# Output projections of a two-layer decoder trunk: four column groups, and two pairs of column groups computed as seven block products

## The chip, the cores and the metric

The kernel runs on one core of a Trainium2 chip. The metric is the device time of one execution in microseconds. Times are compared as medians of several executions; where the text argues from a profile, it uses the one execution that the hardware profiler recorded.

The engines go by short names: PE is TensorE (matrix products; PEld its weight loads), DVE is VectorE, ACT is ScalarE, POOL is GpSimd. SP issues most transfers; each issuing engine has its own queue of instructions and works it off in order.

## The reference, cut to what matters

Each of two layers normalises x (512 tokens, 2048 features, float32), projects it to 6656 columns, mixes tokens in three branches (retention, differential attention, RG-LRU with a convolution), multiplies each by a gate, and projects the 2048 mixed features back:

```python
for l in range(DEPTH):                       # DEPTH = 2
    h = rms_norm(x, pre_norm_g[l])
    proj = jnp.einsum('bsd,de->bse', h, w_in[l])
    (rq, rk, rv, rg, dq, dk, dv, dg, lx, lg) = jnp.split(proj, split_idx, axis=-1)
    ...
    lru_out = rg_lru(lx, ...) * jax.nn.silu(lg)
    mixed = jnp.concatenate([ret_out, diff_out, lru_out], axis=-1)
    y = jnp.einsum('bse,ed->bsd', mixed, w_out[l])
    x = x + rms_norm(y, post_norm_g[l])
```

## The kernel before

All large products keep nearly float32 precision by splitting each operand into a high part (`hi`, rounded to the fast matmul format) and the rest (`lo`), and adding three matmuls: hi x hi, hi x lo, lo x hi. The activations' parts stay on the chip (`hhi`/`hlo` for the normalised x, `mhi`/`mlo` for mix, one pair per 128 features). The weights come from DRAM in chunks of 256 rows x 512 columns (512 KB): `load_chunk` (lines 154 to 166) loads `raw` through SP's queue, rounds it to `whi` on ACT (line 164) and subtracts to get `wlo` on DVE (line 165). There are three buffers of each (`WBUFS`), and `ensure` asks for chunks two ahead of their use.

A pass (`run_pass`, lines 191 to 232) is one group of 512 columns: 8 chunks, 4 banks of results (`big`, in PSUM), 2 x 3 matmuls of 512 columns for each chunk and bank (line 209), 192 in all. The last two chunks are taken bank by bank, so that results come out one after another. There are 13 input passes a layer, in forms A (weights stationary, features come out on the partitions) and B (activations stationary, tokens come out on the partitions). The output projection is four passes of form B over `WO[0]` to `WO[3]`; the last runs as two half passes of two token blocks each, with its weights loaded twice.

Token mixing is written as generators in a list (`side`); `pump` takes one step of the first generator after every second group of matmuls. So the order of the code is the order in which each engine's queue is filled; loads and splits are put some way ahead by a priority, and every engine then works its queue in order. Among the generators are `diff_final`, `ret_final` and `lru_final`, which write `mhi` and `mlo`, and the LRU gates `lg`/`lgs` (lines 661 to 667). Six kinds of 512-column products (lines 633, 643, 666, 736, 818, 931) run on POOL.

`evac_y` (lines 787 to 811) takes a result bank of the output projection: a sum of squares on ACT, a product with `pg` (post-norm gain) on DVE. With the fourth group it forms the norm's factor (`sy`, then `ry` by a power on POOL) and calls `finish` (lines 813 to 836): y x ry + `xr`, where `xr` is the residual read again from DRAM. In layer 0 the result goes to `xs` in DRAM and is transposed for the next layer (`hT`, `hhi`, `hlo`); in layer 1 it is the output.

## Time and profile before

| | us |
|---|---|
| median of 3 runs | 1642.38 (1642.27 to 1642.62) |
| the profiled execution | 1641.9 |
| its span | 1640.1 |
| output projection of layer 0, first to last large matmul | about 639 to 820 |
| output projection of layer 1 | about 1458 to 1631 |
| end of the last matmul to the end of the span | 8.8 |

A line of the profile's groups has the line of the kernel, the engine, the operation, result <- operands by the program's names, the shape, the count, then busy time and mean duration in ns, then the engine's idle time just ahead of these instructions and what ended it. Matmuls overlap, so that their durations add up to more than their time. A line of the chain has start, length, engine and what. The rows that carry the argument stand in the prediction.

### The profile page before, as it was taken

What the parts mean: (1) busy time and instruction counts of PE and PEld (TensorE: products, weight loads), DVE (VectorE), ACT (ScalarE), POOL (GpSimd) and SP (SyncE); (2) the same over time, 40 slices, a digit from 0 to 9 for tenths busy, and PEclk for the clock granted to TensorE, in tenths of its full rate; (3) what the DMA queues carried; (4) which work ended last, traced back from release to release, by engine and by line L of the source; (5) the groups of instructions that cost most, each with busy time, mean ns of one, the idle gap of its engine ahead of it and who ended that gap; (6) DMA issues with size and microseconds to landing.
All of it is one profiled execution on the core that took longest, in us unless ns stands there. A gap on an engine that the chain in (4) does not pass through costs nothing.

```text
span 1640.1 us, 19400 instructions
## 1 busy us (share of the span) xinstructions
PE 1623.5 (99%) x7541; PEld 1342.6 (82%) x7541; DVE 902.8 (55%) x1506; ACT 656.5 (40%) x1024; POOL 133.1 (8%) x136
## 2 busy tenths in 40 slices
PE   9999999999999999999999999999999999999997
PEld 7888888888888888888788888887888888888885
DVE  7747756556477444323762774656756644443236
ACT  7233345456633223222752343435662222332233
POOL 1010001001100120000120000101110001100003
PEclk9999999999999999999999999999999999999999
...
GB/s 229 123 97 103 91 103 55 95 77 97 84 97 102 79 65 96 97 185 135 212 154 97 97 94 93 67 82 78 104 84 96 98 64 83 92 103 97 212 122 193
DMA packets 54748, 177.51 MB, mean 108 GB/s; under 512 B 6656, under 2 KB 7680, under 8 KB 54656
## 3 DMA queue, kind: packets, MB, share of 16 engines
...
q14 instruction: 33, 0.27, 0.1%
q10 hardware_dynamic: 144, 0.04, 0.0%
...
## 4 chain that ended last, share of the span: by engine, by line
PE 93%; DVE 3%; issue 2%; ACT 1%; POOL 1%; DMA 0%; DVEq 0%; POOLq 0%; ACTq 0%
PE big L209 86%; PE gate L622 1%; DVE wlo L165 1%; PE acc L515 1%; PE ro L709 1%; PE rs L684 1%; PE ro L712 0%; PE kv L698 0%; PE sc L483 0%; PE sc L482 0%; PE wT L505 0%; ACT whi L164 0%; PE hT L828 0%; DVE y L820 0%; PE rT L739 0%
## 5 line engine op out<-in xcount | busy, mean ns | idle before, releaser
L165 DVE TENSOR_TENSOR wlo<-raw,whi 128x1024 fp32r<-128x1024 f32 (+1 forms) x289 | 354.5, 1230 | 447.8 <-ACT whi L164 441.3
L164 ACT CAST whi<-raw 128x1024 fp32r<-128x1024 f32 (+1 forms) x289 | 302.4, 1048 | 599.9 <-PE big L209 487.3
L209 PE MATMUL big<-hhi,whi 128*128 128x512 f32 x1024 | 402.0, 393 | 0.5 <-DVE lg L663 0.5
L209 PE MATMUL big<-hlo,whi 128*128 128x512 f32 x1024 | 399.1, 390 | 0.0
L209 PE MATMUL big<-hhi,wlo 128*128 128x512 f32 x1024 | 398.9, 390 | 0.0
L209 PE MATMUL big<-whi,hhi 128*128 128x512 f32 x640 | 253.1, 398 | 0.7 <-ACT whi L164 0.7
L209 PE MATMUL big<-whi,hlo 128*128 128x512 f32 x640 | 249.7, 390 | 0.0
L209 PE MATMUL big<-wlo,hhi 128*128 128x512 f32 x640 | 249.7, 391 | 0.0
L209 PEld LDWEIGHTS big<-hhi,whi 128*128 128x128 f32 x1024 | 192.4, 188 | 40.6 <-DVE lg L663 0.9
L209 PEld LDWEIGHTS big<-hhi,wlo 128*128 128x128 f32 x1024 | 192.2, 188 | 40.1
L209 PEld LDWEIGHTS big<-hlo,whi 128*128 128x128 f32 x1024 | 192.5, 188 | 39.1
L209 PE MATMUL big<-wlo,mhi 128*128 128x512 f32 x512 | 199.7, 391 | 1.2 <-DVE wlo L165 1.2
L209 PE MATMUL big<-whi,mhi 128*128 128x512 f32 x512 | 199.9, 390 | 0.0
L209 PE MATMUL big<-whi,mlo 128*128 128x512 f32 x512 | 199.8, 390 | 0.0
L209 PEld LDWEIGHTS big<-wlo,hhi 128*128 128x128 f32 x640 | 120.2, 188 | 25.7
L209 PEld LDWEIGHTS big<-whi,hhi 128*128 128x128 f32 x640 | 120.3, 188 | 24.5 <-ACT whi L164 1.3
L209 PEld LDWEIGHTS big<-whi,hlo 128*128 128x128 f32 x640 | 120.4, 188 | 23.8
L209 PEld LDWEIGHTS big<-wlo,mhi 128*128 128x128 f32 x512 | 96.1, 188 | 22.4 <-DVE wlo L165 2.5
L209 PEld LDWEIGHTS big<-whi,mhi 128*128 128x128 f32 x512 | 96.1, 188 | 20.1 <-ACT whi L164 0.4
L209 PEld LDWEIGHTS big<-whi,mlo 128*128 128x128 f32 x512 | 96.1, 188 | 19.4
L491 ACT ACTIVATE pr<-sc,mx 128x128 f32<-128x128 f32 (+3 forms) x64 | 33.2, 524 | 71.8 <-DVE mx L488 71.7
L417 DVE TENSOR_TENSOR rt<-qk,sin_d 32x512 f32<-32x512 f32 x64 | 43.7, 683 | 3.5 <-ACT qk L459 2.5
...
## 6 DMA issues: line engine op xcount, KB each, us to landing
raw<-in_w_in SPq DMA_DIRECT2D x207, 512.0 KB, 3.6
raw<-in_w_out SPq DMA_DIRECT2D x80, 512.0 KB, 3.4
xT<-in_xt SPq DMA_DIRECT2D x16, 256.0 KB, 6.6
xr<-in_x SPq DMA_DIRECT2D x16, 256.0 KB, 5.7
xs<-y POOLq DMA_DIRECT2D x16, 256.0 KB, 3.5
xr<-xs SPq DMA_DIRECT2D x16, 256.0 KB, 5.6
pg<-in_postg SPq DMA_DIRECT2D x8, 256.0 KB, 3.8
out<-y POOLq DMA_DIRECT2D x8, 256.0 KB, 6.0
```

The lines of the kernel that those rows point to most:

```text
L164: last_copy[0] = A.copy(hi[:, a:b, :], raw[:, a:b, :])
L165: V.tensor_tensor(lo[:, a:b, :], raw[:, a:b, :], hi[:, a:b, :], op=ALU.subtract)
L209: T.matmul(ps[b], lhsT=lhsT, rhs=rhs, start=(cnt[b] == 0), stop=(cnt[b] == total - 1))
L417: V.tensor_tensor(t2[b:b + w, :], raw[a:a + w, :], sin[a:a + w, :], op=ALU.mult)
L491: A.activation(p[:, :n], sc[c][:, :n], AF.Exp, bias=mx[:, c:c + 1], scale=0.125, accum_out=sums[:, h:h + 1])
L515: T.matmul(accs[i][:, h * P:(h + 1) * P], lhsT=wt[:, kb * P:(kb + 1) * P], rhs=dv[kb][:, h * P:(h + 1) * P], start=(kb == 0), stop=(kb == i))
L622: T.matmul(ps[:BW, :], lhsT=wt[:BW, cols], rhs=at[:BW, :], start=(n == 0), stop=(n == 2))
L684: T.matmul(ps[:, n * P:(n + 1) * P], lhsT=k[:, n * P:(n + 1) * P], rhs=q[:, n * P:(n + 1) * P], start=True, stop=True)
L709: T.matmul(po[:, n * P:(n + 1) * P], lhsT=sT[:, n * P:(n + 1) * P], rhs=v[:, n * P:(n + 1) * P], start=True, stop=(n == 0))
```

## The change

The four column groups of an output projection are taken as two pairs (`Pair`, `run_pair`). With A the mix (512 tokens x 2048 features) and B the weights of a pair (2048 rows x 1024 columns), both are cut in 2 x 2 blocks, and the four blocks of the result come from seven block products where eight were computed: A11 B11, A12 B21, A22 T4, S4 B22 and S1 T1, S2 T2, S3 T3, with S1 = A21 - A22, S2 = A11 - S1, S3 = A11 - A21, S4 = A12 - S2 and T1 = B11 + B12, T2 = T1 + B22, T3 = B12 + B22, T4 = T2 + B21. One product is four *units* of 12 matmuls of 512 columns (256 rows of weights, two token blocks), so a pair has 28 units, 336 matmuls. `UNITS` and `UNITS_HALF` are the orders of the units in a layer's first and second pair.

The sums of weights: `pair_unit` keeps B11 in tiles `wx` and adds to it on DVE (T1, T2, T4); T3 is formed by a transfer of POOL's that adds to what is in `raw`. The units are staged: load six units ahead of use (`LOAD`), add four ahead (`ADD`), split two ahead (`SPLIT`). The sums of mix (`Sums.make`, 16 per layer): DVE forms `sf` in float32, ACT and DVE split it into `sp` (two buffers), POOL writes it to DRAM (`sums_out`), and SP reads it back as `s` (four buffers) for each pair. They are made chunk by chunk as `mixed` hands over the last of the four tiles that a chunk needs. The results of the products are combined in `evac` on DVE, three of the seven after a copy by ACT (`held`).

Beside this: the input passes stand in another order (the list `seq` below); v and the gates go to DRAM after their pass (`vg`, `dgs`) and are read back for each head through POOL's queue; layer 1's first pass (`HalfPass`) runs in two halves of two token blocks, with its weights loaded twice; all of POOL's 512-column products but `xsq` run on DVE; `pg`, `xr` and two small loads go through POOL's queue in place of SP's; `NU`, the number of general 512-column buffers, is 63 for 77. The host permutes the columns of `w_in` and the rows of `w_out` to suit. The second pair of layer 0 transposes two token blocks at a time (`turn`).

The first place is DVE's queue at the start of layer 0's output projection. Before, at the end of the last input pass (`dgs`, `dod`, `mlo` belong to differential attention) and with the first splits of the output weights:

```order
L564 SCALAR_TENSOR_TENSOR dgs_5075<-big_4687,rstd,dgs_5075 128x512
L570 TENSOR_TENSOR dod_2782<-dod_2782,dgs_5075 128x512
L578 SCALAR_TENSOR_TENSOR mlo_5088<-dT_5082,subg,mhi_5087 128x512
L578 SCALAR_TENSOR_TENSOR mlo_5097<-dT_5091,subg,mhi_5096 128x512
L578 SCALAR_TENSOR_TENSOR mlo_5106<-dT_5100,subg,mhi_5105 128x512
L578 SCALAR_TENSOR_TENSOR mlo_5115<-dT_5109,subg,mhi_5114 128x512
L165 TENSOR_TENSOR wlo_5126<-raw_5124,whi_5125 128x1024
L165 TENSOR_TENSOR wlo_5156<-raw_5154,whi_5155 128x1024
```

And of the change, with the unit S1_T1 of chunk 1 (`wlo_5417`) and, further on, other units' sums and splits (`wx_4880`, `wx_4881`, `wlo_5440`), the last LRU tiles (`lh`) and their low parts:

```order
L217 TENSOR_TENSOR wlo_5417<-wx_4945,whi_5416 128x512
L217 TENSOR_TENSOR wlo_5417<-wx_4946,whi_5416 128x512
L953 TENSOR_TENSOR lh_3074<-lh_3074,lgs_5198 128x512
L953 TENSOR_TENSOR lh_3620<-lh_3620,lgs_5229 128x512
L258 TENSOR_TENSOR wx_4880<-wx_4880,raw_5457 128x512
L258 TENSOR_TENSOR wx_4881<-wx_4881,raw_5457 128x512
L217 TENSOR_TENSOR wlo_5440<-raw_5272,whi_5439 128x1024
L1034 TENSOR_TENSOR mlo_5298<-lh_3074,mhi_5297 128x512
L953 TENSOR_TENSOR lh_3642<-lh_3642,lgs_5248 128x512
L1034 TENSOR_TENSOR mlo_5303<-lh_3620,mhi_5302 128x512
```

Before, only splits follow the last `mlo`, one for each chunk; now splits, weight sums and the last parts of mix stand between each other.

The second place is PE's queue there, in the change. `big_5282` and `big_5289` are the results of A11_B11, `big_5422` and `big_5429` those of S1_T1:

```order
L414 MATMUL big_5422<-wlo_5417,s_5414 128x512
L414 MATMUL big_5422<-whi_5416,s_5414 128x512 x2
L414 MATMUL big_5422<-wlo_5417,s_5414 128x512
L414 MATMUL big_5429<-wlo_5417,s_5414 128x512
L414 MATMUL big_5429<-whi_5416,s_5414 128x512 x2
L414 MATMUL big_5429<-wlo_5417,s_5414 128x512
L414 MATMUL big_5282<-whi_5307,mhi_5297 128x512
L414 MATMUL big_5289<-whi_5307,mhi_5297 128x512
L414 MATMUL big_5282<-whi_5307,mlo_5298 128x512
```

The unit of S1_T1's chunk 1 (operand `s_5414`), and that of chunk 0 before it, now stand ahead of the last unit of A11_B11, which needs the `mlo` of the rows above.

The third place is DVE's queue at the end of layer 1. Before:

```order
L165 TENSOR_TENSOR wlo_12303<-raw_12301,whi_12302 128x1024
L165 TENSOR_TENSOR wlo_12321<-raw_12319,whi_12320 128x1024
L794 SCALAR_TENSOR_TENSOR sy_12345<-ssy,msy 128x1
L797 TENSOR_TENSOR y_12343<-big_12227,pg_12047 128x512
L820 SCALAR_TENSOR_TENSOR y_11469<-y_11469,ry_12347,xr_11845 128x512
L820 SCALAR_TENSOR_TENSOR y_11727<-y_11727,ry_12347,xr_11847 128x512
```

And of the change, with `wlo_13076` the last split of the kernel, and `e` and `held` the results of token blocks 0 and 1:

```order
L217 TENSOR_TENSOR wlo_13056<-wx_12348,whi_13055 128x512
L1093 SCALAR_TENSOR_TENSOR e_12603<-e_12603,ry_13021,xr_12700 128x512
L1069 TENSOR_TENSOR held_12799<-held_12799,pg_12445 128x512
L1093 SCALAR_TENSOR_TENSOR e_12413<-e_12413,ry_13043,xr_12723 128x512
L1091 TENSOR_TENSOR held_12791<-held_12791,xr_12702 128x512
L1093 SCALAR_TENSOR_TENSOR held_12047<-held_12047,ry_13043,xr_12725 128x512
L1093 SCALAR_TENSOR_TENSOR e_12617<-e_12617,ry_13043,xr_12727 128x512
L1091 TENSOR_TENSOR held_12799<-held_12799,xr_12729 128x512
L217 TENSOR_TENSOR wlo_13076<-wx_12367,whi_13075 128x512
L217 TENSOR_TENSOR wlo_13076<-wx_12368,whi_13075 128x512
```

Before, the finishing of token blocks 2 and 3 follows the last split, and that of blocks 0 and 1 stands five splits ahead of it; now seven rows of finishing blocks 0 and 1 stand right ahead of the last split.

The diff, cut to its core:

```diff
-NU = 77
+NU = 63
 WBUFS = 3
+RBUFS = 4
+SBUFS = 4
+PBUFS = 2
+IN_PAIRS = (False, False)
+SPLIT, ADD, LOAD = 2, 4, 6
...
+class Pair:
+    def __init__(self, w1, w2, act, sums, out1, out2, order=None):
+        self.w, self.act, self.sums, self.out = (w1, w2), act, sums, (out1, out2)
+        self.order = order or UNITS
+        self.x, self.kept = {}, {}
...
+A11_B11, A12_B21, S1_T1, S2_T2, S4_B22, S3_T3, A22_T4 = range(7)
+SUM_OF = {S1_T1: 0, S2_T2: 1, S4_B22: 3, S3_T3: 2}
+ALONE = [[(s, c) for c in range(4)] for s in range(7)]
+def _both(s, t):
+    return [(u, c) for c in range(4) for u in (s, t)]
+UNITS = ALONE[A11_B11] + _both(S1_T1, S3_T3) + _both(S2_T2, S4_B22) + _both(A12_B21, A22_T4)
+UNITS_HALF = ALONE[A11_B11] + ALONE[A12_B21] + _both(S1_T1, S3_T3) + _both(S2_T2, S4_B22) + ALONE[A22_T4]
...
+    def two(tag, s, dt=F32):
+        return wp.tile([P, 2, S], dt, tag=tag, name=nm(s), bufs={"raw": RBUFS, "s": SBUFS, "sp": PBUFS}.get(tag, WBUFS))
...
+    def pair_unit(n, p, s, c):
+        w1, w2 = p.w
+        if s == A11_B11:
+            src = p.x[c] = [U("wx"), U("wx")]
+            for kk in range(2):
+                nc.sync.dma_start(src[kk], w1[c][:, kk * S:(kk + 1) * S])
+        elif s == S1_T1:
+            p.kept[c] = load_raw(w2[c])
+        elif s == S2_T2:
+            p.kept[c] = load_raw(w2[c + 4])
+        elif s == A12_B21 or s == A22_T4 and p.order is not UNITS:
+            p.kept[c] = load_raw(w1[c + 4])
+        yield
+        if s in (S1_T1, S2_T2, A22_T4):
+            src = p.x[c]
+            for kk in range(2):
+                V.tensor_tensor(src[kk], src[kk], p.kept[c][:, kk, :], op=ALU.add)
+        elif s == S3_T3:
+            src = p.kept[c]
+            nc.gpsimd.dma_start(src, w2[c + 4].rearrange("p (k c) -> p k c", k=2), accum_op=ALU.add)
+        elif s != A11_B11:
+            src = p.kept[c]
+        yield
+        sums = None
+        if s in SUM_OF:
+            sums = two("s", "s", F32R)
+            nc.sync.dma_start(sums.bitcast(F32), p.sums.dram[SUM_OF[s], c])
+        hi, lo = split_tiles()
+        if isinstance(src, list):
+            for kk in range(2):
+                split(hi[:, kk, :], lo[:, kk, :], src[kk])
+        else:
+            split(hi, lo, src)
+        unit_tiles[n] = hi, lo, sums
...
+    def ensure(i, ahead=True):
+        for step, more in enumerate((LOAD - SPLIT, ADD - SPLIT, 0)):
+            while reached[step] <= min(i + (more if ahead else 0), len(units) - 1):
+                n = reached[step]
+                p, u = units[n]
+                if n not in steps:
+                    steps[n] = pair_unit(n, p, *u) if isinstance(p, Pair) else unit(n, p, u) if n else first_unit(p)
+                if step == 2 and isinstance(p, Pair) and u[0] in SUM_OF:
+                    until(lambda: (SUM_OF[u[0]], u[1]) in p.sums.written)
+                with tc.high_priority(HP):
+                    next(steps[n])
+                reached[step] += 1
...
+        def evac(s, t, x):
+            o1, o2 = p.out
+            if s in (A11_B11, S1_T1, S3_T3):
+                held = {A11_B11: p1, S1_T1: p5, S3_T3: p7}[s]
+                held[t] = U("held")
+                A.copy(held[t], x)
+            elif s == A12_B21:
+                e = U("e")
+                V.tensor_tensor(e, x, p1[t], op=ALU.add)
+                o1(t, e)
+            elif s == S2_T2:
+                w, e = U("w"), U("e")
+                V.tensor_tensor(w, x, p1[t], op=ALU.subtract)
+                V.tensor_tensor(p5[t], p5[t], w, op=ALU.add)
+                V.tensor_tensor(e, p5[t], p7[t], op=ALU.subtract)
+                V.tensor_tensor(p7[t], p7[t], w, op=ALU.subtract)
+                o2(2 + t, e)
+            elif s == S4_B22:
+                V.tensor_tensor(p5[t], x, p5[t], op=ALU.add)
+                o2(t, p5.pop(t))
+            else:
+                V.tensor_tensor(p7[t], x, p7[t], op=ALU.add)
+                o1(2 + t, p7.pop(t))
...
+            if s in (A11_B11, A12_B21):
+                k = 2 * c + (0 if s == A11_B11 else 8)
+                until(lambda: k in p.act and k + 1 in p.act)
+            ensure(base + n + SPLIT)
+            hi, lo, sums = unit_tiles.pop(base + n)
+            for t in range(2):
+                if c == 0:
+                    ps[s, t] = pb.tile([P, S], F32, tag="big", name=nm("big"))
+                for kk in range(2):
+                    ah, al = (stationary(s, c, kk, part, sums)[:, t * P:(t + 1) * P] for part in range(2))
+                    for m, (wt, at) in enumerate(((hi, ah), (hi, al), (lo, ah))):
+                        T.matmul(ps[s, t], lhsT=at, rhs=wt[:, kk, :], start=(c == kk == m == 0),
+                                 stop=(c == 3 and kk == 1 and m == 2))
+                if c == 3:
+                    with tc.high_priority(HP):
+                        evac(s, t, ps.pop((s, t)))
+            pump(2)
...
+                if n == 0:
+                    minus(t[:, cols], a21, a22)
+                elif n == 1:
+                    minus(t[:, cols], a11, made[c, 0][:, cols])
+                elif n == 2:
+                    minus(t[:, cols], a11, a21)
+                else:
+                    minus(t[:, cols], a12, made[c, 1][:, cols])
...
+            parts = two("sp", "sp", F32R)
+            A.copy(parts[:, 0, :], t)
+            yield
+            V.tensor_tensor(parts[:, 1, :], t, parts[:, 0, :], op=ALU.subtract)
+            nc.gpsimd.dma_start(self.dram[n, c], parts.bitcast(F32))
+            self.written.add((n, c))
...
+    def mixed(l, st, k, m):
+        hi, lo = U("mhi", F32R), U("mlo", F32R)
+        A.copy(hi, m)
+        V.tensor_tensor(lo, m, hi, op=ALU.subtract)
+        st["mix"][k] = (hi, lo)
+        st["mf"][k] = halves(m)
+        c = k % 8 // 2
+        if all(n in st["mf"] for n in (2 * c, 2 * c + 1, 2 * c + 8, 2 * c + 9)):
+            sums_side.append(st["sums_out"].chunk(c))
...
+            here = [m for m in range(4) if (tb, m) in st["y"]]
+            if len(here) == 4:
...
+            elif len(here) == 4 and tb % 2:
+                for q in (0, 2, 1, 3):
+                    for t in (tb - 1, tb):
+                        finish(l, st, t, q)
+                    turn(l, st, tb // 2, q)
+                side.append(squares(st, (tb - 1, tb)))
...
-            G.tensor_tensor(y, y, xr, op=ALU.add)
+            V.tensor_tensor(y, y, xr, op=ALU.add)
...
-        seq = [
-            (B_(C_DV, evac_dv(st), l > 0), []),
-            (A_(C_DQ, lambda b, ps, st=st: evac_rope(st, ps, st["dq"], b, "dq")), []),
-            (A_(C_DK, lambda b, ps, st=st: evac_rope(st, ps, st["dk"], b, "dk")),
-             [lambda st=st, l=l: diff_attention(l, st)]),
-            (A_(C_LX, ev_l(st, 0)), [lambda st=st, l=l: lru_half(l, st, 0)]),
-            (A_(C_LX + 512, ev_l(st, 4)), [lambda st=st, l=l: lru_half(l, st, 1)]),
-            (A_(C_LX + 1024, ev_l(st, 8)), [lambda st=st: lru_final(st)]),
-            (A_(C_RQ, ev_rq(st, 0)), []),
-            (A_(C_RQ + 512, ev_rq(st, 4)), []),
-            (A_(C_RQ + 1024, ev_rq(st, 8)), []),
-            (B_(C_RV, evac_rvg(st, [("v", 0), ("v", 1), ("v", 2), ("v", 3)])),
-             [lambda st=st, l=l: ret_all(l, st, range(4))]),
-            (B_(C_RV + 512, evac_rvg(st, [("v", 4), ("v", 5), ("g", 0), ("g", 1)])),
-             [lambda st=st, l=l: ret_all(l, st, (4, 5))]),
-            (B_(C_RV + 1024, evac_rvg(st, [("g", 2), ("g", 3), ("g", 4), ("g", 5)])),
-             [lambda st=st: ret_final(st, range(6))]),
-            (B_(C_DG, evac_dg(st)), [lambda st=st, l=l: diff_final(l, st)]),
...
+            seq = [
+                (HalfPass(W[G_DV], st["h"], out_dv(st)) if l else plain(G_DV, out_dv(st)), []),
+                dq, dk,
+                (plain(G_V, out_vg(l, 0, S)), []),
+                (plain(G_DG, out_dg(l)), []),
+                lx, lx1,
+                (plain(G_G, out_vg(l, 1, 0)), []),
+                (A_(G_R0, ev_r(st, 0)), [lambda st=st, l=l: ret_all(l, st, (0, 1))]),
+                (plain(G_VG, out_vg(l, 2, 256)), []),
+                (A_(G_R1, ev_r(st, 1)), [lambda st=st, l=l: ret_all(l, st, (2, 3))]),
+                (A_(G_R2, ev_r(st, 2)), [lambda st=st, l=l: ret_final(l, st, (0, 1, 2, 3)),
+                                         lambda st=st, l=l: ret_all(l, st, (4, 5)),
+                                         lambda st=st, l=l: ret_final(l, st, (4, 5))]),
+                lx2,
+            ]
+        seq += [
...
+            (Pair(WO[0], WO[1], st["mix"], st["sums_out"], out_y(l, st, 0), out_y(l, st, 1)), []),
+            (Pair(WO[2], WO[3], st["mix"], st["sums_out"], out_y(l, st, 2), out_y(l, st, 3), UNITS_HALF), []),
```

566 lines of the change are left out of this document (359 added, 207 removed).

## The prediction

> **What bounds the kernel now.** I read the page's busy times first, then its chain, then the costliest groups.
>
> ```profile
> span 1640.1 us, 19400 instructions
> PE 1623.5 (99%) x7541; PEld 1342.6 (82%) x7541; DVE 902.8 (55%) x1506; ACT 656.5 (40%) x1024; POOL 133.1 (8%) x136
> PE 93%; DVE 3%; issue 2%; ACT 1%; POOL 1%; DMA 0%; DVEq 0%; POOLq 0%; ACTq 0%
> L209 PE MATMUL big<-whi,mhi 128*128 128x512 f32 x512 | 199.9, 390 | 0.0
> L209 PE MATMUL big<-wlo,mhi 128*128 128x512 f32 x512 | 199.7, 391 | 1.2 <-DVE wlo L165 1.2
> ```
>
> TensorE (PE) is busy for 99% of the span, and 93% of the chain that ends last is its work. The 390 ns of a row is not its price, since matmuls overlap. The price is in long pieces of the chain of waits (start, length, what):
>
> ```profile
> 431.75 106.08 PE big L209 x468
> 643.33 145.34 PE big L209 x641
> ```
>
> 106.08 / 468 = 0.2267 us for a matmul of 512 columns, and the second piece, inside layer 0's output stage, gives the same. A unit of the new plan (12 matmuls) is thus 2.72 us. What the other engines do in the output stages stands in the view by windows (window, length, then busy time and count of PE, PEld, DVE, ACT, POOL, then clock, DMA share, GB/s):
>
> ```profile
> 640.00:720.00 80.00, 80.00 (x357) 66.03 (x356) 24.64 (x24) 21.55 (x29) 0.00 (x0) 1.00 0.36 119
> 720.00:800.00 80.00, 79.78 (x358) 65.73 (x358) 34.03 (x45) 28.34 (x46) 4.08 (x7) 1.00 0.54 179
> 800.00:840.00 40.00, 39.22 (x198) 31.93 (x197) 35.17 (x84) 34.60 (x98) 7.14 (x13) 1.00 0.57 188
> 1540.00:1620.00 80.00, 79.47 (x351) 65.33 (x350) 35.75 (x44) 27.28 (x37) 8.69 (x12) 1.00 0.54 180
> ```
>
> VectorE (DVE) is 31 to 45% busy there and PE never waits; at the turn of the layers (800 to 840) DVE and ACT are near 90% and PE still loses only about 1 us. So the output stages have free vector time, some 50 us in each 80, and the change spends it. Whether it fits is the whole question.
>
> **The change part by part.** *Fewer matmuls.* Each layer's output projection goes from 4 x 192 = 768 matmuls to 2 pairs x 28 units x 12 = 672, so 192 fewer in all: 192 x 0.2267 = **-43.5 us**. All input projections keep their matmuls.
>
> *Vector work of a pair.* A row's duration is not what it takes from DVE when independent work follows:
>
> ```profile
> L165 DVE TENSOR_TENSOR wlo<-raw,whi 128x1024 fp32r<-128x1024 f32 (+1 forms) x289 | 354.5, 1230 | 447.8 <-ACT whi L164 441.3
> 817.32 0.75 DVE L820 SCALAR_TENSOR_TENSOR y<-y,ry,xr 128x512 f32<-128x512 f32 x1 [0.23 <-POOL ry L796]
> ...
> 819.64 1.21 DVE L165 TENSOR_TENSOR wlo<-raw,whi 128x1024 fp32r<-128x1024 f32 x1
> 820.78 0.68 DVE L797 TENSOR_TENSOR y<-big,pg 128x512 f32<-128x512 f32 x1
> 821.38 1.21 DVE L165 TENSOR_TENSOR wlo<-raw,whi 128x1024 fp32r<-128x1024 f32 x1
> ```
>
> The starts lie 1.14 us apart after the 1024-wide split and 0.60 after the 512-wide product, which I take as prices (0.66 for a row with two operations and 0.33 for 256 columns are estimates in proportion). A pair has 28 splits (16 as two halves: 32 x 0.60; 12 whole: 12 x 1.14), 24 sums of weights, 14 combinations of products and 8 scalings with `pg`: 19.2 + 13.7 + 14.4 + 8.4 + 4.8 = 60.5 us, against 28 x 2.72 = 76.2 us of PE. On average it fits (79%). It doesn't at the start of a layer's first pair, where the last gates of the LRU and the sums of mix land as well. By the new order, with `lg` at 0.60, DVE has 17.0 us of rows in units 0 to 3 (24 x 0.60 + 8 x 0.33), then 13.7, 10.9, 7.7, 7.7, 13.7 and 5.3, and PE 10.9 in each four. The first eight units are 30.7 against 21.8: 8.9 us over.
>
> Little of that can be done ahead: there are three buffers for weight parts, and the two splits before the pair sit in the last slots of the pass before. The page's waits show that this binds already:
>
> ```profile
> ACT whi L164 <- PE big L209: 487.3, 167, 5.4
> raw<-in_w_out SPq DMA_DIRECT2D x80, 512.0 KB, 3.4
> xs<-y POOLq DMA_DIRECT2D x16, 256.0 KB, 3.5
> xr<-xs SPq DMA_DIRECT2D x16, 256.0 KB, 5.6
> out<-y POOLq DMA_DIRECT2D x8, 256.0 KB, 6.0
> ```
>
> The split's first half waits for PE to free a buffer 167 times, 487 us in all. I walked the rows from the pair's first matmul (0 us), each beginning when DVE is free and its inputs are there. S1_T1's unit 1 has its `wlo` (`wlo_5417`) at 13.9 where PE wants it at about 11.9: 2.0 us lost. The last `mlo` of A11_B11's chunk 3 (`mlo_5303`) is nine rows on, behind a split and two weight sums: 4.5 lost in all. The next split makes it 5.5. Then S1_T1's chunk 3 needs the sum `s_5504`: its low part (`sp_5338`) is ready at 27.4, is written to DRAM and read back, while PE wants it at 32.7. No row shows that round trip; the write lies between 3.5 (256 KB) and 12 (twice 6.0), the read between 3.4 and 11.2 (twice 5.6), so the trip is 6.9 to 23.2 us. I take 4.5 + 4.0 = 8.5, near the rows with 512 KB and POOL's 3.5: 35.9, so PE has lost about 8.8 when its own lateness is counted. The burst of combinations at units 20 to 23 (13.7 against 10.9) adds 1.2 after what the light units before it gain. The four accumulating loads of S3_T3 are the other operation without a row, at 3.4 to 12 us by the same rows; POOL issues each four units, 10.9 us, before its product, of which the split takes some 2, so I take 0 (at 12 the first would cost 3). That is **10 us for each layer's first pair** (3 to 17: the least if the order lets only the last `mlo` bind, the most with the trip at 16), both layers alike: **+20**.
>
> The Trainium skill ("DMA: Bandwidth & Descriptors", "Anatomy of one DMA — SWDGE (gpsimd) path") has 2.0 us and a share by size for a GpSimd transfer, which makes 3.2 for 512 KB and 6.4 for write and read. By that my sum would be some 4 us lower; the trace's 3.5 for half the bytes speaks for the longer trip.
>
> *Turn of the layers.* The second pair's end carries the finishing of x and its transposes as before, plus the combinations. Units 24 to 27 hold 17.7 us of DVE rows against 10.9, and the next pass is now in two halves with 16 units of 2.72 us for one pass of eight. In the window 800 to 840 the same mixture cost 1 us at 88%; here it is above 100% for some 11 us. I take **+3** (0 to 6.8, the whole excess).
>
> *End of layer 1.* Behind the middle of unit 22 DVE has 28 rows of 512 columns and 6 tiny ones (row below: 0.16) to the last split, `wlo_13076`: 22 x 0.60 + 6 x 0.66 + 6 x 0.15 = 18.1 us. PE reaches that weight after 4.5 units and five matmuls, 13.4 us. **+4.7** (0 to 6; none if the finishing of the first blocks overlaps more). The tail after the last matmul:
>
> ```profile
> 1630.88 0.39 PE L209 MATMUL big<-wlo,mhi 128*128 128x512 f32 x1
> 1632.09 0.16 DVE L794 SCALAR_TENSOR_TENSOR sy<-ssy,msy 128x1 f32<-128x1 f32 x1 [0.19 <-ACT junk L790]
> 1632.16 0.68 DVE L797 TENSOR_TENSOR y<-big,pg 128x512 f32<-128x512 f32 x1
> 1632.91 3.08 DVE L820 SCALAR_TENSOR_TENSOR y<-y,ry,xr 128x512 f32<-128x512 f32 x3
> 1633.74 1.71 POOL L818 TENSOR_TENSOR y<-y,xr 128x512 f32<-128x512 f32 x1 [0.87 <-ACT y L817]
> ```
>
> It is 1640.1 - 1631.3 = 8.8 us. Two additions of held products and the last block's fourth sum (was POOL, now DVE) come in: +3 x 0.60. The three finishing rows, 1.03 each beside POOL's product where the one at 817.32 took 0.75 without it, give back 0.8: **+1.0** (-0.5 to 2).
>
> *Input stage.* 48 products leave POOL for DVE, the dearest group being
>
> ```profile
> L666 POOL TENSOR_TENSOR lgs<-lgs,lg 128x512 f32<-128x512 f32 x12 | 17.9, 1495 | 84.3 <-ACT lgs L665 84.2
> L823 POOL DMA_DIRECT2D xs<-y x16 | 9.0, 562 | 17.3 <-DVE hlo L836 11.9 <-DVE y L820 5.4
> ```
>
> About 48 x 0.60 = 29 us of DVE over 1200 us, with 40 copies on ACT, the trips of v and gates through DRAM, and eight more chunk loads and splits. POOL trades its products (1.5 us each) for DMA issues (0.56 each), those of the loads moved off SP among them, and is 8% busy and off the chain, DVE stays below 84% in the busiest pass by the same row prices and ACT below 92%, so PE's work hides it: **+1** (0 to 10, if a pass with 92% behaves like the first pair).
>
> Sum, against the profiled execution's 1641.9: -43.5 + 20 + 3 + 4.7 + 1.0 + 1 = -13.8, so **1628.1**. The median of the three runs is 0.5 higher (1642.38), so 1628.6.
>
> **The rivals.**
>
> *Vector work hides (about 1609).* For it: 79% on average, and 88% cost only 1 us before. Then each first pair loses 3, the turn 0, the end 3: 1641.9 - 43.5 + 6 + 3 + 1 + 1 = 1609.4. Against it: the 8.9 us over are in the order, and only two splits can be ahead.
>
> *The trip of the sums through DRAM decides (about 1650, slower).* A sum is made on DVE, split on ACT and DVE, written by POOL and read by SP; the next reads, and the raw weights of later units, stand behind it in SP's queue. In the first 45 us of a pair some 30 transfers of 512 KB are asked for, 15.7 MB or 340 GB/s, where the fastest stretch of the trace moved
>
> ```profile
> 9.00:12.00 3.00, 3.00 (x15) 2.49 (x14) 2.77 (x4) 2.65 (x5) 0.00 (x0) 1.00 1.03 396
> 1631.00:1640.00 9.00, 0.27 (x2) 0.00 (x0) 4.74 (x6) 1.41 (x3) 2.60 (x3) 0.79 0.59 209
> ```
>
> 396 GB/s at full use. The other terms leave 43.5 - 9.7 = 33.8 us for the two first pairs, so the case decides from 17 us in each, that is a trip of 15.5 in place of 8.5. At 20 us of trip, 21 each: 1641.9 - 43.5 + 42 + 9.7 = 1650. Against it: most trips start earlier than the one I priced, and 512 KB of weights land in 3.4.
>
> *The clock falls in the gaps (about 1636).* Before, PE had no gap after its start, and the granted clock was 1.00; in the last 9 us, with PE nearly idle, it was 0.79 (row above). Start-up shows the price:
>
> ```profile
> 1.39 3.75 PE L950 MATMUL warm<-warm 128*128 128x512 bf16 x9 [1.39 <-POOL warm L947]
> ```
>
> 0.42 us a matmul for 3.75 us, against 0.2267: a fall costs about 1.7 us. My stalls are 1 to 3.3 us, one or two a pair long enough to count; four or five falls add 8: 1636. Page "TensorE: Matmul & The Clock Gate" of the Trainium skill (Part 1: The HAM clock gate (the "warmup" mystery)) sets the fall after an idle window of about 3.4 us; by that rule the short stalls of the first units cost nothing, and only the 3.3 us one and the last are near it. The 0.79 agrees with the direction.
>
> *The matmul count doesn't fall.* The order shows 192 fewer rows of 512 columns, so this has no chance worth naming.
>
> **How the numbers follow.** My forecast (1619 to 1638) gets 0.50, the hidden case (1605 to 1619) 0.24, the clock 0.10, the trip 0.16 (1638 to 1660). The range leaves out about a tenth on either side: 1607 to 1648. A measurement of this kernel tells 0.2% from no change, that is 3.3 us: faster below 1639.1, slower above 1645.7. Faster: 0.49 + 0.24 + 0.07 = 0.80; same: 0.01 + 0.02 + 0.04 = 0.07; slower: 0.01 + 0.12 = 0.13.
>
> **What would show it.** Right: 6336 matmuls of 512 columns; in each first pair PE idle 8 to 12 us, released by DVE's `wlo`, `mlo` and by the read of `s`; DVE's share above 90% in the pair's first 25 us, near 70% behind; idle of 4 to 5 us before the last unit. The forecast is wrong if PE's idle time in the first pairs is under 4 us (hidden), if most of it is released by a DMA (trip), if the granted clock falls under 0.95 in an output window, or if an input pass loses over 5 us.

## The result, and the profile after

The changed kernel takes 1705.54 us (median; 1704.15 to 1706.88) where the kernel before takes 1642.33 (median of 4): ratio 1.039, 95% interval 1.0376 to 1.0403. It is 63 us slower, with 192 matmuls fewer. The forecast was 1628.6 us and the range ended at 1648.

The page of the changed kernel, its lines on busy time, the costliest groups of the pairs, and the transfers (KB each, median us from issue to landing):

```profile
span 1705.1 us, 20087 instructions
PE 1615.6 (95%) x7349; PEld 1315.2 (77%) x7349; DVE 1094.1 (64%) x1846; ACT 746.2 (44%) x1178; POOL 166.8 (10%) x254
L414 PE MATMUL big<-whi,s 128*128 128x512 f32 x512 | 165.1, 406 | 22.0 <-DMA s<-sums_out 15.5
L414 PE MATMUL big<-whi,mlo 128*128 128x512 f32 x192 | 77.3, 403 | 8.7 <-DVE mlo L1034 8.7
L414 PE MATMUL big<-wlo,mhi 128*128 128x512 f32 x192 | 76.4, 406 | 5.8 <-DVE wlo L217 5.7
s<-sums_out SPq DMA_DIRECT2D x64, 512.0 KB, 8.1
raw<-in_w_out SPq DMA_DIRECT2D x56, 512.0 KB, 6.6
sums_out<-sp POOLq DMA_DIRECT2D x32, 512.0 KB, 3.7
raw<-in_w_out POOLq DMA_DIRECT2D x16, 512.0 KB, 8.2
```

PE, which waited for next to nothing before, now sits idle ahead of groups that read sums of mix, late parts of mix and late weights. The weights of the output projection land in 6.6 us where they took 3.4. The same windows show it (columns as in the prediction):

```profile
660.00:680.00 20.00, 15.06 (x55) 10.97 (x53) 16.80 (x26) 7.21 (x12) 3.14 (x4) 0.85 0.85 229
700.00:720.00 20.00, 19.37 (x85) 15.36 (x84) 12.59 (x17) 8.91 (x13) 0.00 (x0) 1.00 0.90 335
770.00:775.00 5.00, 2.51 (x8) 1.73 (x7) 3.76 (x6) 2.21 (x5) 2.14 (x4) 0.79 1.04 343
785.00:790.00 5.00, 5.00 (x24) 4.14 (x23) 1.32 (x2) 1.14 (x2) 0.00 (x0) 1.00 1.02 393
1620.00:1640.00 20.00, 16.93 (x72) 13.11 (x72) 12.34 (x23) 6.12 (x11) 8.30 (x15) 1.00 1.04 364
```

Three things are new: the transfer engines are full for long stretches (share 0.85 to 1.04), PE has holes, and the granted clock falls to 0.79 to 0.85 around them.

To see where the time went I followed PE's timeline from the start of one matmul to the start of the next and took off 0.2267 us for 512 columns, and for the smaller ones what most of their kind take. What is left is lost time. It is in the table by stage; a part is idle time that the timeline marks with what ended it, the rest is mostly slow matmuls.

| stage | lost before | lost after | idle part after | forecast to add |
|---|---|---|---|---|
| input passes, layer 0 | 14.0 | 29.7 | 12.0 | 1 in both |
| first pair, layer 0 | 0.4 | 16.5 | 9.8 | 10 |
| second pair, layer 0, and first pass of layer 1 | 3.9 | 29.2 | 16.1 | 3 |
| other input passes, layer 1 | 12.1 | 28.9 | 12.6 | (above) |
| first pair, layer 1 | 0.4 | 15.6 | 9.9 | 10 |
| second pair, layer 1 | 2.3 | 20.3 | 14.4 | 4.7 |
| after the last matmul | 8.8 | 12.7 | | 1 |

("First pair" of before is the first 336 matmuls of the projection.) The additions make 111 us; less 43.5 for the matmuls that went, 67.5, against 65.0 between the spans. The missing 2.5 us are the error of this count: no matmul record is missing (PE has 7349, 192 fewer than the 7541 before), so they lie in what was taken off for the smaller matmuls.

### The profile page after: what moved, and what is told of

The parts are those of the page before. It is cut to its first block, busy times and chain, and to the rows that moved or that the text cites. A ratio compares the mean times of both kernels' runs of the same rounds, so it can differ in the third digit from the quotient of the medians.

```text
span 1705.1 us, 20087 instructions
## 1 busy us (share of the span) xinstructions
PE 1615.6 (95%) x7349; PEld 1315.2 (77%) x7349; DVE 1094.1 (64%) x1846; ACT 746.2 (44%) x1178; POOL 166.8 (10%) x254
## 5 line engine op out<-in xcount | busy, mean ns | idle before, releaser
L217 DVE TENSOR_TENSOR wlo<-raw,whi 128x1024 fp32r<-128x1024 f32 (+1 forms) x265 | 322.1, 1218 | 274.9 <-ACT whi L216 268.6
L326 PE MATMUL big<-whi,hhi 128*128 128x512 f32 x576 | 226.4, 395 | 5.9 <-DVE lx L939 5.7
L414 PE MATMUL big<-whi,s 128*128 128x512 f32 x512 | 165.1, 406 | 22.0 <-DMA s<-sums_out 15.5
L414 PEld LDWEIGHTS big<-whi,s 128*128 128x128 f32 x512 | 98.7, 196 | 49.1 <-issue 15.5
L216 ACT CAST whi<-wx 128x512 fp32r<-128x512 f32 x128 | 73.9, 617 | 72.3 <-PE big L414 67.2
L414 PE MATMUL big<-wlo,s 128*128 128x512 f32 x256 | 101.9, 401 | 0.3 <-DVE wlo L217 0.3
L217 DVE TENSOR_TENSOR wlo<-wx,whi 128x512 fp32r<-128x512 f32 x128 | 83.4, 685 | 21.6 <-ACT whi L216 19.6
L258 DVE TENSOR_TENSOR wx<-wx,raw 128x512 f32<-128x512 f32 x96 | 62.9, 687 | 53.3 <-DMA raw<-in_w_out 53.1
L414 PE MATMUL big<-whi,mlo 128*128 128x512 f32 x192 | 77.3, 403 | 8.7 <-DVE mlo L1034 8.7
L414 PE MATMUL big<-wlo,mhi 128*128 128x512 f32 x192 | 76.4, 406 | 5.8 <-DVE wlo L217 5.7
```

What stands on the lines that cost most here:

```text
L216: last_copy[0] = A.copy(hi, raw)
L217: V.tensor_tensor(lo, raw, hi, op=ALU.subtract)
L258: V.tensor_tensor(src[kk], src[kk], p.kept[c][:, kk, :], op=ALU.add)
L326: T.matmul(ps[b], lhsT=lhsT, rhs=rhs, start=(c == kk == n == 0), stop=(c == 7 and kk == 1 and n == 2))
L414: T.matmul(ps[s, t], lhsT=at, rhs=wt[:, kk, :], start=(c == kk == m == 0), stop=(c == 3 and kk == 1 and m == 2))
```

## The experiments

Seventeen kernels. All but `e8_clock`, which computes no trunk, start from the changed kernel, `e13` to `e15` from its version without sums of mix (`e9`). `e6`, `e9` and `e12` to `e15` leave out part of the computation. The kernel before, run beside each, took 1640.3 to 1641.8 us. A difference of 2 to 3 us between kernels timed on different occasions can't be told from none: the kernel before alone moved from 1642.3 to 1640.3.

**The change's input stage alone** (`e1_plain_out`): four plain output passes in place of the pairs, with three raw buffers and 69 general ones.

```diff
-        seq += [(Pair(WO[0], WO[1], ...), []), (Pair(WO[2], WO[3], ..., UNITS_HALF), [])]
+        seq += [(make(0), []), (make(1), []), (make(2), []), (HalfPass([WO[3][c] for c in PERM], Perm(st["mix"]), out_y(l, st, 3)), [])]
```

> The change's input stage with four plain output passes (six-row-block order of chunks, last group in two halves), no block products and no sums. Theory A, the input stage loses by itself (PE idle 12 to 13 us in each layer plus slow clock behind each gap): about 1674 us, 1668 to 1682, with the gaps at the LRU gates and the last retention heads still there. Rival, the input stage only suffers from the sums and transfers of the pairs that reach back into it: 1640 to 1652, and no gap over 2 us before the output passes.

1654.42 us, between the two. The input passes of layer 0 take some 6 us more than before, those of layer 1 some 8, the tail 3, and the gaps at the LRU gates of layer 0 are gone. So new order, DRAM trips and products on DVE cost about 14 us, and the pairs cost 51 on top of them although they save 43.5. Some of the pairs' cost lies in the input passes.

**What holds the input passes.** In layer 0, PE waits 4.6 us for `lx` to empty a result bank. The timelines of ACT and DVE there:

```profile
341.60 4.20 ACT L910 ACTIVATE gt<-gate,pp 32x512 f32<-32x512 f32 x6
344.42 2.10 DVE L914 TENSOR_TENSOR gt<-gt,xc 128x512 f32<-128x512 f32 x3 [6.53 <-ACT gt L910]
345.82 1.28 ACT L920 ACT_TABLE_LOAD   x1
348.49 0.69 DVE L924 TENSOR_TENSOR gt<-la 128x512 f32<-128x512 f32 x1 [1.96 <-ACT lt L922]
352.69 0.68 DVE L939 TENSOR_TENSOR lx<-big,rsb 128x512 f32<-128x512 f32 x1
```

DVE waits in its queue for ACT's gates, and `lx` stands behind, and PE behind that (us in total, times, longest):

```profile
PE big L326 <- DVE lx L939: 5.7, 2, 4.6
```

At the last retention heads the load of the gate is issued by POOL behind a power, and DVE waits 4.34 us for it:

```profile
631.86 1.01 POOL L998 TENSOR_TENSOR rf<-rss,mhalf 128x4 f32<-128x4 f32 x1 [5.52 <-DVE rss L996]
632.83 1.58 POOL L842 DMA_DIRECT2D rvg<-vg  x2
639.40 0.69 DVE L1020 TENSOR_TENSOR ro<-ro,rvg 128x512 f32<-128x512 f32 x1 [4.34 <-DMA rvg<-vg]
```

PE's waits behind it, in both layers:

```profile
PE rT L1024 <- DVE ro L1020: 9.3, 4, 4.5
```

Two edits, one for each place (`e2_gates_pool`, `e3_gate_early`):

```diff
-            V.tensor_tensor(gates[1][j], gates[1][j], xc[j], op=ALU.mult)
+            G.tensor_tensor(gates[1][j], gates[1][j], xc[j], op=ALU.mult)
...
-            V.tensor_tensor(a2, a, a, op=ALU.mult)
+            G.tensor_tensor(a2, a, a, op=ALU.mult)
```

> Only the two kinds of LRU gate products (24 of 512 columns) go back from DVE to POOL. Theory A, DVE stood in its queue waiting for ACT's gates with the emptying of PE's result banks behind it: the gaps at the second gate half of each layer (4.8 + 1.2 and 5.3 us, and some 1.7 us of slow clock behind each) go, 1705 - 13 = 1692 us, 1688 to 1696. Rival, ACT's own twelve gate functions in a row delay the banks whoever multiplies: over 1701.

1702.96 us; the waits for `lx` and for ACT's `e` stay (4.4 and 5.2 us). The theory fell: DVE now waits 11.72 us for POOL in the same place, since ACT finishes the gates when it did. Who multiplies doesn't matter, as the rival said; the 2.6 us less are within the noise.

```diff
     def ret_all(l, st, heads):
         v = load_vg(l, heads[0], 0)
+        if heads[0] == 4:
+            for h in heads:
+                st["rg"][h] = load_vg(l, h, 1)
...
```

> Only the gate loads of retention heads 4 and 5 are issued at the start of their retention instead of one step before use. Theory A, the load stood behind the power on POOL's queue and took its 6 us round trip in PE's path: gaps of 4.7 and 4.2 us with 1.3 and 2.5 us of slow clock go, 1705 - 10 = 1695 us, 1692 to 1699. Rival, the pair behind is limited by its own vector work and waits that much longer: over 1702.

1697.39 us: 8 less, and the wait for `ro` falls from 4.9 and 4.4 us to 0.4. The theory held.

**Bandwidth, or order in a queue?** In the stretch of S1_T1 and S3_T3, two units (5.44 us) ask for two weight transfers (one of them accumulating) and two sums, 2 MB, which is 385 GB/s. On the other hand SP's timeline shows this at the start of layer 0's second pair:

```profile
736.19 26.37 SPq L209 DMA_DIRECT2D raw<-in_w_out  x5
```

Five weight loads take 26 us to be issued, because their buffers are not free (SP waits for the splits that free them, up to 15.9 us at a time), and reads of sums stand behind them. Five runs were to tell the two apart. `e4_xr_early` moves the residual's loads ahead, into the A12_B21 units:

```diff
-                run_pair(p, {(S1_T1, 1): lambda st=st, l=l: load_x(l, st, 0),
-                             (A22_T4, 1): lambda st=st, l=l: load_x(l, st, 1)})
+                run_pair(p, {(A12_B21, 0): lambda st=st, l=l: load_x(l, st, 0),
+                             (A12_B21, 2): lambda st=st, l=l: load_x(l, st, 1)})
```

> Only the loads of the residual move from the seven-product part of the second pair to its first half, where the transfer engines were idle. Theory A, the second pair is short of transfer bandwidth for some 50 us (4 MB of residual beside 8 MB of sums and 8 MB of weights): the waits for sums of 4.9 and 9.2 us halve and the waits for the residual at the turn go, 1705 - 18 = 1687 us, 1680 to 1694. Rival, the sums are late because weight loads that wait for buffers stand ahead of them in SP's queue: over 1700, with the waits for sums above 3 and 7 us.

1715.82 us, 10 slower: over 1700, as the rival had it, but neither theory had foreseen a loss. The waits for sums in the second pairs grow to 11.3 and 12.6 us, while at the turn the wait of 6.7 us for finishing goes. It looks as if the loads pressed on the sums' reads where they went, and freed the place they left. `e12_no_xr` leaves them out:

```diff
-                t = U("xr")
-                nc.gpsimd.dma_start(t, src[tb * P:(tb + 1) * P, n * S:(n + 1) * S])
-                st["xr"][tb, n] = t
+                st["xr"][tb, n] = junk2
```

> The residual is not read and zeros are added in its place (the output is not the reference's): 4 MB a layer less in the second pairs. Theory A, the turn's waits (6.7 us for finishing, 2.6 for its transposes, 7 of slow clock) are late residual loads, and they also press on the sums: first pass of layer 1 from 63 to 50 us, second pairs 4 less each, 1705 - 21 = 1684 us, 1677 to 1692. Rival, the finishing itself (DVE rows in its queue, two block transposes at once) holds PE at the turn: 1697 or more and a first pass over 58 us.

1687.43 us, within the range of the first theory: second pair of layer 0 from 89.0 to 84.0 us, first pass of layer 1 from 63.1 to 57.0 (50 expected), waits for sums 3.1 and 3.7. In the changed kernel the chain is plain in the waits:

```profile
DVE held L1093 <- DMA xr<-in_x: 6.9, 3, 4.9
PE hT L1107 <- DVE held L1093: 6.6, 3, 3.8
```

`e6_half_s` reads half of each sum back:

```diff
-            nc.sync.dma_start(sums.bitcast(F32), p.sums.dram[SUM_OF[s], c])
+            nc.sync.dma_start(sums[:, :, :256].bitcast(F32), p.sums.dram[SUM_OF[s], c][:, :, :256])
...
-                return sums[:, part, kk * 256:(kk + 1) * 256]
+                return sums[:, part, 0:256]
```

> Of each sum of mix only one half (256 of 512 columns, 256 KB of 512) is read back, and that half is used twice; the output is not the reference's. Theory A, transfer bandwidth: 2 MB per two units (385 GB/s) in the S1_T1 and S3_T3 stretch becomes 1.5 MB (290 GB/s), the waits for sums in the second pairs (4.9 and 9.2 us) and the waits for the residual at the turn (6.7 us) shrink to a third and the slow clock behind them with them: 1705 - 25 = 1680 us, 1672 to 1690. Rival, order in SP's queue (the reads stand behind weight loads that wait for buffers): over 1697, the waits for sums above 3 and 6 us.

1693.34 us: 12 less, between the theories. PE's wait for sums over the whole run (us in total, times, longest) in the changed kernel:

```profile
PE big L414 <- DMA s<-sums_out: 15.5, 9, 3.0
```

And with half the bytes:

```profile
PE big L414 <- DMA s<-sums_out: 11.3, 5, 3.9
```

The first read of each second pair still comes 3.5 and 3.9 us late, at half the bytes: so it isn't its own bytes that delay that one, and its place in SP's queue, behind the weight loads, is the likely cause. `e10_s_pool` therefore issues the reads from POOL:

```diff
-            nc.sync.dma_start(sums.bitcast(F32), p.sums.dram[SUM_OF[s], c])
+            nc.gpsimd.dma_start(sums.bitcast(F32), p.sums.dram[SUM_OF[s], c])
```

> Only the queue from which the sums are read back changes: POOL's in place of SP's. Theory A, order: in SP's queue the reads stand behind weight loads that wait up to 20 us for a buffer; the waits for sums in the second pairs (4.9 and 9.2 us) halve with their slow clock: 1705 - 10 = 1695 us, 1690 to 1699. Rival, bandwidth: the same bytes in the same stretch, 1702 to 1710.

1742.91 us, 37 slower, which neither theory had. The reads, which wait for PE to free a buffer, now hold up the accumulating transfers in POOL's queue; DVE's additions wait for them, and behind these the splits and `mlo`:

```profile
POOL s L268 <- PE big L414: 100.9, 41, 5.5
DVE wx L258 <- DMA raw<-in_w_out: 107.1, 34, 7.4
PE big L414 <- DVE wlo L217: 26.0, 19, 4.0
PE big L414 <- DVE mlo L1034: 16.2, 2, 8.5
```

PE's waits for sums do fall (5.8 us in all for 15.5; 4.1 more have no releaser in the trace) and a sum lands sooner (5.5 us for 8.1), as the order theory had it, but all else came later, so that the run doesn't tell how much is order and how much bytes. `e7_units2` gives the second pair the order of the first, with four weight loads fewer:

```diff
-            (Pair(WO[2], WO[3], ..., out_y(l, st, 2), out_y(l, st, 3), UNITS_HALF), []),
+            (Pair(WO[2], WO[3], ..., out_y(l, st, 2), out_y(l, st, 3)), []),
```

> Only the order of units in the second pair changes to that of the first: four weight loads (2 MB) fewer in each second pair, but all four token blocks end at the pair's end. Theory A, bandwidth presses on the second pairs: their waits for sums fall from 4.9 and 9.2 to under 3 and 6 us, but the finishing of all blocks in one place gives that back at the turn and at the end: 1700 to 1712 us, with the second pair's waits for sums lower. Rival, the loads don't matter: waits for sums unchanged and the time over 1712.

1705.69 us. The wait for sums in the second pair of layer 0 goes (from 4.9 to under 0.4) and that in layer 1 falls to 3.9, but first pass of layer 1 grows from 63.1 to 66.4: given back at the finishing, as expected.

**The first pair.** DVE's timeline of the changed kernel, and PE's behind it:

```profile
669.38 1.28 DVE L953 TENSOR_TENSOR lh<-lh,lgs 128x512 f32<-128x512 f32 x2
672.62 1.29 DVE L258 TENSOR_TENSOR wx<-wx,raw 128x512 f32<-128x512 f32 x2 [1.95 <-DMA raw<-in_w_out]
673.83 1.22 DVE L217 TENSOR_TENSOR wlo<-raw,whi 128x1024 fp32r<-128x1024 f32 x1
674.97 0.68 DVE L1034 TENSOR_TENSOR mlo<-lh,mhi 128x512 fp32r<-128x512 f32 x1
675.71 0.79 PE L414 MATMUL big<-whi,mlo 128*128 128x512 f32 x1 [4.20 <-DVE mlo L1034]
676.30 0.63 PE L414 MATMUL big<-wlo,mhi 128*128 128x512 f32 x1
676.73 0.63 PE L414 MATMUL big<-whi,mhi 128*128 128x512 f32 x1
677.15 0.63 PE L414 MATMUL big<-whi,mlo 128*128 128x512 f32 x1
```

The wait for the last `mlo` is there, and half of it is not DVE's work: DVE waits 1.95 us for a weight load in front of an addition. Behind the gap matmuls start 0.43 us apart. `e5_units` puts one more unit between:

```diff
-UNITS = ALONE[A11_B11] + _both(S1_T1, S3_T3) + ...
+FIRST = [(A11_B11, 0), (A11_B11, 1), (A11_B11, 2), (S1_T1, 0), (S1_T1, 1), (A11_B11, 3), (S1_T1, 2), (S3_T3, 0),
+         (S3_T3, 1), (S1_T1, 3), (S3_T3, 2), (S3_T3, 3)]
+UNITS = FIRST + ...
```

> Only the order of units in a layer's first pair changes: one unit of S1_T1 goes ahead of the last unit of A11_B11 at most two in DVE's queue as well, and one stands between it and the first unit of S3_T3. Theory A, the last low part of mix was late for PE because weight work stood ahead of it and the copies of A11_B11's results came just when S3_T3 needed the banks: the waits of 4.2 and 2.4 us and two slow-clock stretches of about 2 us go in each layer, 1705 - 18 = 1687 us, 1683 to 1693. Rival, DVE is simply full in the first eight units, so that the wait only moves to the next split: 1700 or more, the first pair within 3 us of its 92.

1706.94 us, the first pair 92.7 as it was. The wait for `mlo` falls to 0.6 us, but the copy that empties A11_B11's banks is then 6.5 us late: the rival held, the wait only moves.

**The sums left out.** `e9_no_sums` leaves out the sums of mix, `e13_no_sums_no_t` those of the weights as well:

```diff
-                return sums[:, part, kk * 256:(kk + 1) * 256]
+                return p.act[2 * c + kk + 8][part][:, lo_]
...
```

> The sums of mix are left out: products with S take parts of mix instead, so nothing is summed, split, written or read back; the sums of weights, the 336 matmuls a pair and the combinations stay; the output is not the reference's. Theory A, sums of mix are the main cost (their transfers in the second pairs, their DVE and ACT work in the LRU passes and the first pairs): the input passes take what they take with plain output passes (10 and 11 us less), the second pairs lose only their end (about 25 us less), the turn 10 less: about 1645 us, 1635 to 1658. Rival, the sums of weights and the tripled splitting in the pairs are the main cost: over 1670.

1664.54 us: the sums of mix cost 41 us, 19 of it in the input passes (648.9 to 638.0 and 603.8 to 595.4 us) and 19 in the first pairs (92.7 to 82.0 and 91.8 to 83.6). The second pairs hardly gain (89.0 to 88.4): with the sums gone PE waits for `wlo` there. The time lies between the two theories.

```diff
-                V.tensor_tensor(src[kk], src[kk], p.kept[c][:, kk, :], op=ALU.add)
...
-            nc.gpsimd.dma_start(src, w2[c + 4].rearrange("p (k c) -> p k c", k=2), accum_op=ALU.add)
```

> Besides the sums of mix the sums of weights are left out (no additions to wx, no accumulating transfers); matmuls, splits, combinations and finishing stay; the output is not the reference's. Theory A, the sums of weights hold the pairs that are left after the run without sums of mix (82 to 88 us where 76 are matmuls): first pairs 77, second pairs 80 to 84, 1664 - 15 = 1649 us, 1643 to 1655. Rival, bursts of combinations and the finishing hold them: 1657 or more.

1631.38 us, ratio 0.994 (0.992 to 0.997): another 33 us, double what was expected, and the first pairs take 76.3 us, where their 336 matmuls are 76.2. A window of layer 0's first pair in the run without sums of mix:

```profile
660.00:680.00 20.00, 17.32 (x68) 13.49 (x67) 11.76 (x17) 6.98 (x11) 0.57 (x1) 0.91 0.42 127
```

And in the run without either sums:

```profile
660.00:680.00 20.00, 20.00 (x90) 16.57 (x89) 9.84 (x12) 9.92 (x16) 0.00 (x0) 1.00 0.31 102
```

So splits and combinations fit, as the prediction's average had it, and sums don't. Why are the sums of weights so dear, at 14.4 us of DVE a pair? `e14_no_sums_raw6` gives six raw buffers for four, `e15_no_accum` drops the accumulating transfers and keeps the additions; neither has sums of mix.

```diff
-RBUFS = 4
+RBUFS = 6
```

> The run without sums of mix (its output is not the reference's), with six buffers for raw weights where it had four (the room of the sums' split buffers). Theory A, the sums of weights are dear because their additions wait in DVE's queue for weight loads that wait for a buffer (59 us of DVE waiting for raw loads), with the splits behind them: the 33 us between 1664 and 1631 shrink by half, 1648 us, 1640 to 1655. Rival, the additions' own DVE time and the accumulating transfers: over 1658.

> The run without sums of mix, and without the accumulating transfers of T3 as well (the output is not the reference's); the additions on DVE stay. Theory A, late raw loads hold the additions and the accumulating transfers only hold a raw buffer some 7 us longer: part of the 33 us goes, 1664 - 12 = 1652 us, 1645 to 1658. Rival 1, the accumulating transfers are all of it: 1631 to 1637. Rival 2, the additions are all of it: over 1660.

1641.09 and 1637.08 us: 23 and 27 of the 33 us, the second at the edge of its first rival. DVE's waits for raw loads ahead of the additions in the run without sums of mix (`e9`):

```profile
DVE wx L258 <- DMA raw<-in_w_out: 58.9, 30, 5.1
```

And with six buffers (`e14`):

```profile
DVE wx L258 <- DMA raw<-in_w_out: 14.2, 9, 3.3
```

An accumulating transfer lands after 8.2 us (6.8 without sums of mix) and keeps a raw buffer meanwhile; loads for later units wait for that buffer, additions for the loads, splits for the additions. What counts is what arrives at PE: it waits 19.0 us for late splits in the pairs of `e9`, 6.9 in `e14`, 7.9 in `e15` and 4.8 in `e13`. DVE's own wait is no price: it is still 39.1 us in `e15`, the faster of the two. The additions, with what they wait for, are worth the 6 us that `e15` still has over `e13`.

**The change in full, mended.** `e16_mended` has five raw buffers, early gate loads and POOL's products:

```diff
-NU = 63
+NU = 61
...
-RBUFS = 4
+RBUFS = 5
```

> The change in full, with three things mended: five raw buffers and 61 general ones, the gate loads of the last heads issued early, LRU gate products back on POOL. If the three add up: 8 for the gates' loads, 2 for the products, 5 to 12 for the buffer, 1705 - 18 = 1687 us, 1680 to 1694. If the general buffers were needed, the input passes lose more than the pairs win: over 1697. Either way not under 1641.

1696.17 us, 9 less where 18 were expected: little more than the gate loads alone. `e17_raw6` finds room for six raw buffers by keeping the rotary tables in two of them:

```diff
+    def new_tabs():
+        d, r = two("raw", "tabd"), two("raw", "tabr")
+        tabs.update(zip(TABS, (d[:, 0, :], d[:, 1, :], r[:, 0, :], r[:, 1, :])))
...
-RBUFS = 4
+RBUFS = 6
```

> The change in full, with six raw buffers for four: the rotary tables live in two of them during the input passes and give them back for the output projection (nothing is left out). Theory A, the raw buffers that the accumulating transfers hold are what makes the sums of weights dear, here as without the sums of mix: 1705 - 20 = 1685 us, 1679 to 1692, DVE's wait for raw loads in the pairs under half of 53 us. Rival, with the sums of mix on the same queues the loads come no earlier: over 1697.

1699.47 us, 6 less. DVE still waits for raw loads with the sums of mix on the same queues:

```profile
DVE wx L258 <- DMA raw<-in_w_out: 54.4, 25, 5.1
```

The second pairs gain (89.0 to 83.9 us in layer 0, 96 to 88 in layer 1), the first pairs lose (92.7 to 94.9, 92 to 96). The rival held in the time and in DVE's wait: with the sums of mix on the same queues, more raw buffers are worth little, and only in the second pairs. `e17_raw6_gates_late_sums` adds the early gate loads and holds the sums of mix back until the retention passes:

```diff
-            for line in (side, sums_side):
+            for line in ((side,) if hold[0] else (side, sums_side)):
...
+            hold[0] = i < 8
```

> As the run beside it, with the last heads' gate loads early and the sums of mix held back until the retention passes. Theory A, the sums made during the LRU passes push the LRU gates into the emptying of the next pass's banks: the gaps at the LRU gates of layer 0 go (7 us with slow clock) and those at the last heads (8): 15 under the run beside it, 1670 us, 1662 to 1678. Rival, the held sums crowd the last input passes and the first pair: within 8 of the run beside it.

1685.86 us, 13.6 under the run beside it, where 15 were expected; the time itself lies over its range, since the run beside it did. The waits for `lx` and `ro` are gone, and the input passes of layer 0 take 641.9 us for 650.6. It is the fastest version with all of the computation, ratio 1.028 (1.025 to 1.031); none beats the kernel before.

**The clock by itself** (`e8_clock`): bursts of 60 matmuls, the gaps between them made by DVE.

```diff
+            for m in range(60):
+                T.matmul(ps, lhsT=lhs, rhs=rhs, start=(m == 0), stop=(m == 59))
...
+            for q in range(g):
+                V.tensor_tensor(fill[:, :128], fill[:, :128], raw[:, :128], op=ALU.min)
```

> No trunk is computed: bursts of 60 matmuls of 512 columns, with gaps of growing length made by a chain of small DVE operations that the next burst waits for, 16 lengths from about 1 to 6 us, three times each. Theory A, a gap of 2.4 us and more can drop the granted clock, and the next 6 to 10 matmuls take 0.43 instead of 0.227 us (1.3 to 2.5 us lost): none under about 2 us, some between 2.4 and 3.4, all above. Rival (an idle window of about 3.4 us): no slow matmul behind any gap under 3.4 us.

The timeline of PE (start, length of the burst, and the gap before it):

```profile
122.29 13.85 PE L167 MATMUL big<-rhs,lhs 128*128 128x512 f32 x60 [2.43 <-DVE rhs L172]
138.90 15.22 PE L167 MATMUL big<-rhs,lhs 128*128 128x512 f32 x60 [2.76 <-DVE rhs L172]
157.21 13.85 PE L167 MATMUL big<-rhs,lhs 128*128 128x512 f32 x60 [3.09 <-DVE rhs L172]
174.47 15.48 PE L167 MATMUL big<-rhs,lhs 128*128 128x512 f32 x60 [3.41 <-DVE rhs L172]
193.69 16.72 PE L167 MATMUL big<-rhs,lhs 128*128 128x512 f32 x60 [3.74 <-DVE rhs L172]
```

A burst takes 13.85 us at full clock. None of the 18 gaps up to 2.44 us slowed the next burst; those of 2.76 us did three times of three, 3.09 never, 3.41 once of three, and from 3.74 us all 20 did, at 1.4 to 2.9 us each. The first theory held in kind, but length alone draws no border. The trace's granted clock draws it: in this run it falls only at moments that lie whole multiples of 3.413 us apart. Cut the gaps at these moments, and the 24 that slowed a burst have a piece of 1.98 us or more, the 23 others none over 1.90. A gap of 2.76 us had 2.2 to 2.4 us in one piece, one of 3.09 us was cut into 1.3 to 1.4 and 1.7 to 1.8.

## Why the prediction was wrong, point by point

Against the table, the input passes cost 32.5 us where +1 was forecast, the second pairs with the turn 43.3 for +7.7, the first pairs 31.3 for +20, and the tail 3.9 for +1. One term was put at nothing without asking what it holds (the accumulating transfers); the terms that were farthest off were sized by rows of DVE and ACT, not by what waits for a transfer or for a place in a queue.

**The matmuls** went as forecast: 192 fewer, and without any sums the first pairs take what their matmuls take (76.3 us for 76.2).

**Vector work of a pair.** Splits, combinations and scalings fit (`e13`). The sum that had the additions fit as well, 60.5 of 76.2 us, counted DVE's rows and not what they wait for. The step that failed is "so I take 0" for the accumulating transfers: their landing of 8.2 us lies within the bounds given, but what they hold was not asked. They keep one of four raw buffers, and by that the loads, additions and splits behind. Where sums of mix are away, leaving them out gave 27 of 33 us (`e15`), and two more raw buffers 23 (`e14`).

**First pairs**, +10 each: the idle time is 9.8 and 9.9 us, but with another make-up, so that this agreement is in part luck. The last `mlo` took 4.2 of the 4.5 forecast. The sum `s_5504` lost next to nothing, though a trip took longer than the 8.5 us counted (3.7 for the write and 8.1 for the read, medians of the whole run); in its place PE waited 2.4 us for ACT to empty banks. Slow matmuls behind the gaps made it 16.5 and 15.6.

**Input stage**, +1: off by some 31 us. "PE's work hides it" failed by itself: 14 us stay with plain output passes (`e1`). Of the products on DVE, the 24 that were put back were worth nothing clear of noise (`e2`). The sums of mix are also made in these passes, which the term left out: 19 us (`e9`), of which making them later gave back some 6 (13.6 less the gate loads' 8). The gate load behind a power on POOL's queue was 8 (`e3`); this overlaps with the 19, since without sums PE's waits for `ro` are 3.3 us in place of 9.3. That POOL is "off the chain" was read from the trace before, where POOL issued few transfers that anyone waited for.

**Second pairs and turn**, +3 and +4.7: the forecast had no wait for sums after the first pair and none for the residual. For the first pair it added up 340 GB/s of transfers against 396 (15.7 MB in 45 us are 349), for the second, with the residual and the reloaded weights beside the sums, it added nothing up. Measured: 25 and 18 us; without the residual 18 of the kernel's time go (`e12`). The last split's lateness (5.2 us idle, 4.7 forecast) was right. In the tail 2.9 of the 3.9 us stay with plain output passes (`e1`), so that most of it is not the held products that were priced.

**The rivals.** The trip of the sums was the nearest, at 0.16 and 1650 us, with its place in the first pairs; transfers did decide much, but through buffers and queues, and more in the second pairs than in the first. The clock came on top and was priced at 8 us; the changed kernel's granted clock falls twelve times ahead of the end, and the matmuls 0.43 us apart in these stretches lose some 20 us in all, against none before. "TensorE: Matmul & The Clock Gate" of the Trainium skill (Part 1: The HAM clock gate (the "warmup" mystery)) has a window of about 3.4 us that runs free of the kernel. The free-running window agrees with falls at multiples of 3.413 us in `e8_clock`, and with gaps of 2.76 us that slow PE beside 3.09 that don't; by the traces 3.4 us of idle time is no bound from below, since 1.98 us in one piece was enough. So "the short stalls of the first units cost nothing" didn't hold: gaps of 2.4 us were followed by matmuls 0.43 us apart in both first pairs.

Two of the prediction's signs of being wrong came: the granted clock fell to 0.85 in an output window (under 0.95), and the LRU pass of layer 0 lost over 5 us (5.7 us idle).

What stays open: how the remaining loss of the first pairs in `e17_raw6` (95 us for 76) divides between bytes and queue order, as no run took only one of them away there.
